# Masks of the prompt attention's scores: from TensorE products into VectorE's maximum

## The chip, the core and the metric

The kernel runs on one core of a Trainium2 chip. The metric is the device time of one execution in microseconds (us), the median over several runs. A core has five engines with a queue of instructions each: TensorE (PE; its weight loads are listed as PEld), VectorE (DVE), ScalarE (ACT), GpSimd (POOL) and SyncE (SP, which here only issues DMA transfers). Each engine takes its instructions in the order of the program and waits for the others by semaphores. Matrix products write to PSUM banks of 512 columns of fp32; everything else lies in SBUF.

## The reference

One layer of a decoder trunk runs for two groups: a prompt of 1024 tokens and a sample group of 8 sequences with 8 new tokens and 2048 cached ones each. A layer is half a SwiGLU feed-forward, a mixer and another half feed-forward. The mixer joins a Mamba-2 head group and an attention head group of 8 query heads over 2 key/value heads. The attention has three branches, compressed blocks, selected blocks and a sliding window of 512 tokens. With 1024 prompt tokens all 16 blocks are selected, so the prompt's selected branch is plain causal attention. Each branch is a masked softmax:

```python
def masked_softmax(s, mask):
    s = jnp.where(mask, s.astype(jnp.float32), NEG)
    e = jnp.where(mask, jnp.exp(s - jnp.max(s, axis=-1, keepdims=True)), 0.0)
    return e / jnp.maximum(jnp.sum(e, axis=-1, keepdims=True), 1e-30)
```

The selected branch masks keys after the query; the window branch masks those and keys 512 or more tokens back. Scores carry a slope times the distance (ALiBi) as well. For the sample group the compressed branch needs summaries of the cached rows: blocks of 32 rows go through a small two-layer network, per sequence, for keys and for values.

## The kernel before, in words

The program is one long function that goes through stages: first feed-forward, projections and Mamba-2, the prompt's attention (here from 1138 to 1548 us of the span), the sample group's attention together with the output projection (1548 to about 1740), second feed-forward, outputs. Products that need fp32 accuracy are split into high and low parts and made as three products.

**Prompt attention.** The loop goes over 8 tiles of 128 queries in the order `qt` = 2, 7, 6, 5, 4, 3, 1, 0, over two key/value heads g, over two branches br (0 selected, 1 window), and over the four query heads of g. The nk keys that a tile can see (up to 1024 in branch 0, up to 640 in branch 1) are taken in one part, or in two parts if they are more than 512. For a part of pn keys TensorE makes the scores s in one of three PSUM banks (`s2`) with two products, queries times keys (L1808) and ALiBi with the low parts (L1810). Then a mask product (L1813) adds the identity times a 128x128 tile of 0 and -1e30: `mdiag` on the last 128 keys of the last part, `medge` on the first 128 keys of the window when it is full (qt of 4 and more). The parts come to 192, the mask products to 160; 32 parts, the first of two in branch 0, have no mask. VectorE takes the maximum of a part (L1818 for one part; L1821 for each of two and L1822 over the two), and ScalarE makes the exponential from PSUM into the SBUF tile pb with the row sum beside it (L1824). There are five pb tiles per branch; a group of four heads uses four. After the four heads, pb is scaled by gate over sum (L275 to L279, on ScalarE, GpSimd or VectorE by a table), transposed by TensorE (L1846, pT), copied to SBUF (pt), and multiplied with the values into o (L1855). The compressed branch of the prompt (s_cmp, pc) has a mask product of its own (L1770), once per tile of queries.

**Compression of the sample group's cache.** Written between these tiles, by a table `cs` = 3, 0, 2, 1, 1, 0, 1, 0 that says how many sequences are started ahead of each tile of queries, and interleaved with them on all engines. For each of 8 sequences GpSimd issues a gather of the cached rows into chk (L1689, one buffer); then come eight steps of four transposes each: rows are put in order (chp, ScalarE and GpSimd), transposed (cT, L1712, one PSUM bank), split into high (th, ScalarE) and low (tl, VectorE, L1717), and multiplied with the weights w1h and w1l (cA, L1733 to L1735, 12 products per step). After four steps a summary is made (cxh, c).

**Sample attention.** It needs `big`, a tile of biases and constants that is loaded back from DRAM (L1951), the cached window rows (schk, loaded by SP, L2052), the cached selected blocks (schk, 32 gathers by GpSimd, L2048), the residual x (L1892) and w_out (raw, L1900). Their buffers take over SBUF space of the prompt's attention and of the compression. Its scores already use one VectorE instruction that adds a bias, takes the maximum and writes the sum to SBUF (L2080), followed by a read of the accumulator, and exponentials in place (L2090).

**What sets the order.** The order of each queue is made by the framework's scheduler from the order in the text and its own costs of the instructions; it isn't written by hand. An edit to one instruction can therefore move many others, on all engines.

Of the kernel before, what the change touches and what calls it, by code (L numbers as in the profile page):

```python
# [12 lines left out]
BF16 = mybir.dt.bfloat16  # L13
I32 = mybir.dt.int32
AF = mybir.ActivationFunctionType
OP = mybir.AluOpType
AX = mybir.AxisListType

P = 128
# [61 lines left out]
def hybrid_step(ctx: ExitStack, tc: tile.TileContext, *aps):  # L81
    nc = tc.nc
# [82 lines left out]
    identb = C.tile([P, P], BF16, name="identb")  # L165
# [1231 lines left out]
    KB = KV.tile([P, 2, 2, TP], F32R, name="KB")  # L1397
# [181 lines left out]
    Gs.close()  # L1579
    Ds = ExitStack()  # L1580
    AC = Ds.enter_context(pool("attc"))
    mdiag = AC.tile([P, P], BF16, name="mdiag")
    medge = AC.tile([P, P], BF16, name="medge")
    mcmp = AC.tile([P, 8, 64], BF16, name="mcmp")
    for t_ in (mdiag, medge, mcmp):
        nc.gpsimd.memset(t_, 0.0)
    nc.gpsimd.affine_select(out=mdiag, in_=mdiag, pattern=[[-1, P]], compare_op=OP.is_ge, fill=NEG,
                            base=0, channel_multiplier=1)
# [85 lines left out]
    with pool("att", bufs=2) as K, pool("att_ps2", bufs=3, space=PSUM) as PS2, \  # L1674
# [76 lines left out]
        for qi, qt in enumerate(KN["qt"]):  # L1751
# [3 lines left out]
            QBq = QBs[2 * (qi % 2):2 * (qi % 2) + 2]  # L1755
# [8 lines left out]
            s = PS2.tile([P, 512], F32, name="s_cmp", tag="s2")  # L1764
            for h in range(NH):
# [5 lines left out]
                             start=False, stop=True, skip_group_check=True)  # L1771
            sv = s.rearrange("p (h n) -> p h n", h=NH)
            mx = K.tile([P, NH], F32, name="mxc")
# [11 lines left out]
            for g in range(2):  # L1785
                PT = {}
                for br in range(2):
                    k0 = 0 if br == 0 else max(0, qt - 4)
                    nk = P * (qt + 1 - k0)
                    pbs = []  # L1790
                    hs_ = slice(4 * g, 4 * g + 4)
                    ns = (nk + 511) // 512
                    part = K.tile([P, 4, 2], F32, name="part", bufs=4)
                    for hh_ in range(4):
                        pb = K.tile([P, 1024 if br == 0 else 640], F32, name=f"pb{br}", bufs=5)
                        pbs.append(pb)
                        st, parts = 0, []
                        for i in range(ns):
                            pn = P * ((nk // P - st // P) // (ns - i))
                            s = PS2.tile([P, 512], F32, name="s2", tag="s2")[:, :pn]  # L1800
                            parts.append((s, st, pn))
                            kk = slice(P * k0 + st, P * k0 + st + pn)
                            masks = []
                            if st + pn == nk:
                                masks.append((pn - P, mdiag))
                            if br == 1 and qt >= 4 and st == 0:
                                masks.append((0, medge))
                            nc.tensor.matmul(s, QAs[g][:, hh_], KA[:, br, g, kk], start=True, stop=False,  # L1808
                                             skip_group_check=True)
                            nc.tensor.matmul(s, QBq[g][:97, hh_], KB[:97, br, g, kk], start=False, stop=not masks,  # L1810
                                             skip_group_check=True)
                            for j, (c, mk) in enumerate(masks):
                                nc.tensor.matmul(s[:, c:c + P], identb, mk, start=False,  # L1813
                                                 stop=(j == len(masks) - 1), skip_group_check=True)
                            st += pn
                        mx = K.tile([P, 3], F32, name="mx", bufs=4)
                        if ns == 1:
                            nc.vector.tensor_reduce(mx[:, 0:1], parts[0][0], axis=AX.X, op=OP.max, negate=True)  # L1818
                        else:
                            for i in range(2):  # L1820
                                nc.vector.tensor_reduce(mx[:, 1 + i:2 + i], parts[i][0], axis=AX.X, op=OP.max)  # L1821
                            nc.vector.tensor_reduce(mx[:, 0:1], mx[:, 1:3], axis=AX.X, op=OP.max, negate=True)  # L1822
                        for i, (s, st, pn) in enumerate(parts):
                            nc.scalar.activation(pb[:, st:st + pn], s, AF.Exp, bias=mx[:, 0:1],  # L1824
                                                 accum_out=part[:, hh_, i:i + 1])
                    total = part[:, :, 0]
                    if ns == 2:
                        total = sm[:, 1 + br, hs_]
                        nc.vector.tensor_tensor(total, part[:, :, 0], part[:, :, 1], op=OP.add)
                    nc.vector.reciprocal(sm[:, 1 + br, hs_], total)  # L1830
                    nc.vector.tensor_tensor(sm[:, 1 + br, hs_], sm[:, 1 + br, hs_],  # L1831
                                            gates[:, qt, 8 + 8 * br + 4 * g:12 + 8 * br + 4 * g], op=OP.mult)
                    for hh_ in range(4):
                        h, pb = 4 * g + hh_, pbs[hh_]
                        scale(KN["pb"][qi][4 * br + hh_], pb[:, :nk], pb[:, :nk], sm[:, 1 + br, h:h + 1])
                    PT[br] = (pbs, k0, nk // P)
# [696 lines left out]
```

## Time and profile before

| | us |
|---|---|
| median of 3 runs | 2470.73 (2468.52 to 2479.9) |
| the profiled execution | 2475.45, its span 2473.8 |
| TensorE / VectorE / ScalarE / GpSimd busy | 2408.8 / 1744.7 / 1131.2 / 418.3 |
| prompt attention, 1138 to 1548: TensorE / VectorE / ScalarE / GpSimd busy | 397.87 / 264.00 / 265.76 / 159.31 of 410 |
| mean granted clock of TensorE over the span | 0.987 |

The profile is of one execution, and its times are counted from the start of the span. Busy times of TensorE overlap, since its products are pipelined: a product of 256 columns is listed with 0.28 us while the next one starts 0.12 us later. What a product takes from the engine is therefore read from start to start. A wait is written as the waiting engine and line, an arrow, and the engine and line that released it.

### The profile page before, as it was taken

To read this page: it belongs to the slowest core of one execution; us is meant where nothing else is said; L and a number is where in the kernel's file an instruction comes from. 1 tells how busy PE (TensorE), PEld (TensorE's weight loads), DVE (VectorE), ACT (ScalarE), POOL (GpSimd) and SP (SyncE) were. 2 spreads that over 40 slices of the span, in tenths; PEclk is the share of its full clock that TensorE was granted. 3 is DMA by queue.
4 is the path that set the end of the run, shared out by engine and by line. 5 is a ranking of instruction groups with operands and counts; after the bars stand their busy time and mean duration, and the time that the engine had idled before them with its cause. 6 is when DMAs were issued, how large, how long until landed. Compare 5 with 4: busy or idle time off the path is not lost.

```text
span 2473.8 us, 48193 instructions
## 1 busy us (share of the span) xinstructions
PE 2408.8 (97%) x19026; PEld 2222.8 (90%) x19026; DVE 1744.7 (71%) x3673; ACT 1131.2 (46%) x2501; POOL 418.3 (17%) x533
## 2 busy tenths in 40 slices
PE   7999999999999999999999999999999999999998
PEld 6999999999999998997667766677899999999998
DVE  6777776677778855655656666777967676768776
ACT  7544444441133254425666675444545454543113
POOL 0000000011134343333434343111000000001110
PEclk9999999999999999999999998999999999999999
DMA  4334343598652333423110104476235353559654
GB/s 162 134 133 160 130 164 129 175 338 306 230 190 84 126 116 102 119 69 127 40 64 35 69 35 148 130 250 213 89 123 171 120 174 120 174 213 370 238 209 153
DMA packets 230446, 379.07 MB, mean 153 GB/s; under 512 B 18509, under 2 KB 147705, under 8 KB 228812
## 3 DMA queue, kind: packets, MB, share of 16 engines
q1 hardware_dynamic: 210248, 318.02, 37.7%
q0 software_dynamic: 7600, 38.59, 4.5%
q10 hardware_dynamic: 12372, 19.38, 2.2%
q8 instruction: 150, 2.46, 0.4%
q14 instruction: 76, 0.62, 0.1%
HBM read 255.66 MB, written 124.40 MB: 154 GB/s over the span
## 4 chain that ended last, share of the span: by engine, by line
PE 86%; DVE 6%; DMA 4%; ACT 3%; issue 1%; POOL 0%; ACTq 0%; DVEq 0%; POOLq 0%
PE dq L634 6%; PE gY L367 6%; PE dq L633 6%; PE dq L635 6%; PE gY L368 6%; PE gY L366 6%; PE gX L367 5%; PE gX L366 5%; PE gX L368 5%; PE o L1855 3%; PE pT L1846 3%; PE s L1808 1%; PE xbc L250 1%; PE xbc L251 1%; PE xbc L252 1%; PE cA L1733 1%
## 5 line engine op out<-in xcount | busy, mean ns | idle before, releaser
L634 PE MATMUL dq<-db,da 128*128 128x256 f32 (+1 forms) x1232 | 353.2, 288 | 0.3 <-DVE da L270 0.3
L635 PE MATMUL dq<-db,da 128*128 128x256 f32 (+1 forms) x1232 | 352.8, 288 | 0.0
L633 PE MATMUL dq<-db,da 128*128 128x256 f32 (+1 forms) x1232 | 349.8, 288 | 2.7 <-DVE Cc L386 2.2
L642 DVE TENSOR_TENSOR xT<-xT,dq 128x256 f32<-128x256 f32 (+1 forms) x456 | 186.9, 432 | 84.8 <-PE dq L635 83.2
L270 POOL TENSOR_TENSOR ds<-dw 128x512 f32<-128x512 f32 x22 | 29.5, 1341 | 1228.1 <-DVE wlo L270 508.0
L633 PEld LDWEIGHTS dq<-db,da 128*128 128x128 f32 x1232 | 230.5, 189 | 3.3 <-DVE Cc L386 2.5
L635 PEld LDWEIGHTS dq<-db,da 128*128 128x128 f32 x1232 | 232.8, 189 | 0.0
L634 PEld LDWEIGHTS dq<-db,da 128*128 128x128 f32 x1232 | 231.9, 188 | 0.6 <-DVE da L270 0.5
L267 ACT CAST whi<-ws 128x512 fp32r<-128x512 f32 x156 | 96.5, 623 | 205.9 <-PE gY L368 137.6
L270 DVE TENSOR_TENSOR wlo<-raw,whi 128x512 fp32r<-128x512 f32 x184 | 125.5, 687 | 83.9 <-ACT whi L267 83.5
L267 ACT CAST da<-ds 128x512 fp32r<-128x512 f32 x88 | 52.6, 623 | 234.7 <-PE dq L635 93.4
L267 ACT CAST whi<-raw 128x512 fp32r<-128x512 f32 x181 | 112.4, 626 | 72.0 <-PE g L414 19.5
L270 DVE TENSOR_TENSOR wlo<-ws,whi 128x512 fp32r<-128x512 f32 x156 | 106.7, 687 | 42.4 <-ACT whi L267 41.9
L1824 ACT ACTIVATE pb<-s,mx 128x256 f32<-128x256 f32 (+3 forms) x192 | 105.0, 552 | 59.7 <-DVE mx L1822 37.6
L1846 PEld LDWEIGHTS pT<-ident,pb 128*128 128x128 f32 x528 | 59.6, 143 | 45.8 <-issue 40.1
L1821 DVE TENSOR_REDUCE mx<-s 128x1 f32<-128x384 f32 (+2 forms) x128 | 66.6, 536 | 44.0 <-PE s L1813 34.1
L366 PE MATMUL gY<-B3h,whi 128*128 128x256 f32 (+1 forms) x320 | 91.5, 287 | 1.5 <-ACT whi L267 1.4
L366 PE MATMUL gX<-B6h,whi 128*128 128x256 f32 (+1 forms) x320 | 91.3, 286 | 0.9 <-ACT Cc L373 0.9
L367 PE MATMUL gX<-B6h,wlo 128*128 128x256 f32 (+1 forms) x320 | 91.4, 286 | 0.6 <-DVE wlo L270 0.6
L367 PE MATMUL gY<-B3h,wlo 128*128 128x256 f32 (+1 forms) x320 | 91.6, 287 | 0.2 <-DVE wlo L270 0.2
L277 POOL TENSOR_TENSOR pb<-pb,sm 128x640 f32<-128x640 f32 (+7 forms) x70 | 85.1, 1238 | 37.6 <-DVE sm L1831 34.0
L367 PE MATMUL gY<-B2h,wlo 128*128 128x256 f32 (+1 forms) x320 | 91.4, 286 | 0.0
(763 smaller groups left out, 8548.1 us busy)
## 6 DMA issues: line engine op xcount, KB each, us to landing
db<-GD SPq DMA_DIRECT2D x42, 1632.0 KB
GD<-Cc SPq DMA_DIRECT2D x154, 272.0 KB
GD<-his SPq DMA_DIRECT2D x84, 272.0 KB
raw<-in_ffn_wu_dram SPq DMA_DIRECT2D x22, 1024.0 KB
dw<-in_ffn_wd_dram SPq DMA_DIRECT2D x44, 512.0 KB
raw<-in_ffn_wg_dram SPq DMA_DIRECT2D x21, 1024.0 KB
GD<-hp SPq DMA_DIRECT2D x70, 272.0 KB
db<-GD SPq DMA_DIRECT2D x14, 1088.0 KB
```

The lines of the kernel that those rows point to most:

```text
L267: return nc.scalar.copy(out, src) if eng == "a" else ENGINES[eng].tensor_copy(out, src)
L270: ENGINES[eng].tensor_tensor(out, x, y, op=op)
L277: nc.gpsimd.tensor_tensor(out, x, by.to_broadcast(list(x.shape)), op=OP.mult)
L366: nc.tensor.matmul(q, ah[:, k], b_, start=first, stop=False, skip_group_check=True)
L367: nc.tensor.matmul(q, al[:, k], b_, start=False, stop=False, skip_group_check=True)
L368: nc.tensor.matmul(q, ah[:, k], c_, start=False, stop=(k == 3), skip_group_check=True)
L633: nc.tensor.matmul(q, x, bh[:, u, o], start=first, stop=False, skip_group_check=True)
L634: nc.tensor.matmul(q, y, bh[:, u, o], start=False, stop=False, skip_group_check=True)
L635: nc.tensor.matmul(q, x, bl[:, u, o], start=False, stop=(u == np_ - 1), skip_group_check=True)
L642: nc.vector.tensor_tensor(x, x, q, op=OP.subtract if i == 4 else OP.add)
L1824: nc.scalar.activation(pb[:, st:st + pn], s, AF.Exp, bias=mx[:, 0:1], accum_out=part[:, hh_, i:i + 1])
L1846: nc.tensor.transpose(tq_[:kn, P * hh_:P * hh_ + P], src, ident)
```

## The change

The tiles mdiag and medge become the two ends of one tile `mrow` of 640 columns with zeros between. A part that needs a mask gets a slice of it as wide as the part: the last pn columns for the last part of a tile, the first pn columns for the first part of a full window. The mask product is dropped, and the maximum of such a part is taken by VectorE's fused instruction, which adds the mask to the scores, writes the negated sum into pb and takes the minimum of it, the negated maximum. The exponential then reads pb and writes it in place with the scale -1. Parts without a mask keep the plain maximum and the exponential out of PSUM. Of two parts the smaller of the two negated maxima is taken.

```diff
-    mdiag = AC.tile([P, P], BF16, name="mdiag")
-    medge = AC.tile([P, P], BF16, name="medge")
+    mrow = AC.tile([P, 5 * P], BF16, name="mrow")
+    medge, mdiag = mrow[:, :P], mrow[:, 4 * P:]
...
-                            masks = []
+                            mask = None
                             if st + pn == nk:
-                                masks.append((pn - P, mdiag))
-                            if br == 1 and qt >= 4 and st == 0:
-                                masks.append((0, medge))
+                                mask = mrow[:, 5 * P - pn:]
+                            elif br == 1 and qt >= 4 and st == 0:
+                                mask = mrow[:, :pn]
...
-                            nc.tensor.matmul(s, QBq[g][:97, hh_], KB[:97, br, g, kk], start=False, stop=not masks,
+                            nc.tensor.matmul(s, QBq[g][:97, hh_], KB[:97, br, g, kk], start=False, stop=True,
                                              skip_group_check=True)
-                            for j, (c, mk) in enumerate(masks):
-                                nc.tensor.matmul(s[:, c:c + P], identb, mk, start=False,
-                                                 stop=(j == len(masks) - 1), skip_group_check=True)
+                            parts.append((s, mask, pb[:, st:st + pn]))
...
+                        for i, (s, mask, p_) in enumerate(parts):
+                            m_ = mx[:, 1 + i:2 + i] if ns == 2 else mx[:, 0:1]
+                            if mask is None:
+                                nc.vector.tensor_reduce(m_, s, axis=AX.X, op=OP.max, negate=True)
+                            else:
+                                nc.vector.tensor_tensor_reduce(out=p_, in0=s, in1=mask, scale=-1.0, scalar=3e38,
+                                                               op0=OP.add, op1=OP.min, accum_out=m_)
+                        if ns == 2:
+                            nc.vector.tensor_reduce(mx[:, 0:1], mx[:, 1:3], axis=AX.X, op=OP.min)
+                        for i, (s, mask, p_) in enumerate(parts):
+                            nc.scalar.activation(p_, s if mask is None else p_, AF.Exp, bias=mx[:, 0:1],
+                                                 scale=1.0 if mask is None else -1.0, accum_out=part[:, hh_, i:i + 1])
```

The scheduler gives the stage another order. Three places show it; numbers behind names are those of tiles, and `x2` stands for as many equal instructions in a row. First TensorE at the end of the prompt's attention, before: the last products o, and right behind them the sample group's first products.

```order
L1846 MATMUL pT<-ident,pc 64x128 x4
L1855 MATMUL o<-pt,VA 64x512 x2
L1855 MATMUL o<-pt,VAc 64x512
L1985 MATMUL a_ps<-gates,big 128x24
L2064 MATMUL kT_ps<-ident,schk 128x128 x8
```

After: the last products o, and behind them steps of the compression (the first of them are shown), then at their end the same first products.

```order
L1855 MATMUL o<-pt,VA 64x512 x2
L1855 MATMUL o<-pt,VAc 64x512
L1733 MATMUL cA<-th_13755,w1h 128x256
L1734 MATMUL cA<-th_13755,w1l 128x256
L1712 MATMUL cT<-ident,chp 128x128 x4
L1735 MATMUL cA<-tl_13756,w1h 128x256
...
L1743 MATMUL c_17967<-w_179,cxh 127x64 x2
L2096 LDWEIGHTS zrow
L2096 MATMUL so<-oneh,zrow 128x384
L2064 MATMUL kT_ps<-ident,schk 128x128 x8
```

Between the last o and the first kT_ps there now stand 132 products cA and 40 transposes cT, which were interleaved with the attention; before, the last cA stood ahead of the last 20 of the 192 score parts.

Second GpSimd in the same place, before: scalings of pb, the last reorderings chp, and the gathers of the selected blocks among the last scalings.

```order
L267 COPY chp<-chk 128x2x128 x3
L277 TENSOR_TENSOR pb_18160<-pb_18160,sm 128x256
L270 TENSOR_TENSOR pc<-pc,sm 128x512
L267 CAST QA<-QA 64x2x128
L270 TENSOR_TENSOR QB_13184<-qT,QA 64x2x128
L277 TENSOR_TENSOR pb_18199<-pb_18199,sm 128x256
L2048 DMA schk<-in_cache_sel_dram,idx_9814 128x1024
```

After: the last scaling of the whole stage, then the last gather of the compressed cache, its reorderings, and only then the selected blocks.

```order
L277 TENSOR_TENSOR pb_18405<-pb_18405,sm 128x128
L267 COPY chp<-chk 128x2x128
L1963 MEMSET QS 128x512
L1974 MEMSET zrow 32x128
L267 COPY chp<-chk 128x2x128
L1689 DMA chk<-in_cache_cmp_dram,idx 128x4096
L267 COPY chp<-chk 128x2x128 x8
L2048 DMA schk<-in_cache_sel_dram,idx_9814 128x1024 x32
```

The last gather L1689 moved from among the scalings of 640 columns to behind the last scaling of 128, and all 32 gathers L2048 stand behind it.

Third VectorE at a head with two parts, before: two maxima and the one over both, with a subtraction tl and a copy pt between them.

```order
L1821 TENSOR_REDUCE mx<-s_14710 128x1
L1717 TENSOR_TENSOR tl_13754<-cT,th_13753 128x2x256
L1822 TENSOR_REDUCE mx<-mx 128x1
L267 COPY pt<-pT 128x512
L1717 TENSOR_TENSOR tl_13758<-cT,th_13757 128x2x256
```

After, the same kind of head: the maximum of the part without a mask (L1817), the fused instruction of the other part, which is listed as ISA, and its read of the accumulator.

```order
L1817 TENSOR_REDUCE mx<-s_14689 128x1
L1819 ISA pb_14688,mx<-s_14692,mrow 128x512
L1819 ISA mx 128x1
L1822 TENSOR_REDUCE mx<-mx 128x1
L267 COPY pt<-pT 128x512
```

Every masked part now has two instructions on VectorE where there was one. On SP the order around the sample group's first loads is nearly the same, window rows first (L2052 twice), then big and x, with two tiles of w_out (L1900) now ahead of big.

More of the change, by code (lines that the diff above doesn't have):

```diff
@@ L1581, in hybrid_step @@
     AC = Ds.enter_context(pool("attc"))
-    mdiag = AC.tile([P, P], BF16, name="mdiag")
-    medge = AC.tile([P, P], BF16, name="medge")
+    mrow = AC.tile([P, 5 * P], BF16, name="mrow")
+    medge, mdiag = mrow[:, :P], mrow[:, 4 * P:]
     mcmp = AC.tile([P, 8, 64], BF16, name="mcmp")
-    for t_ in (mdiag, medge, mcmp):
+    for t_ in (mrow, mcmp):
         nc.gpsimd.memset(t_, 0.0)
@@ L1800, in hybrid_step @@
                             s = PS2.tile([P, 512], F32, name="s2", tag="s2")[:, :pn]
-                            parts.append((s, st, pn))
                             kk = slice(P * k0 + st, P * k0 + st + pn)
-                            masks = []
+                            mask = None
                             if st + pn == nk:
-                                masks.append((pn - P, mdiag))
-                            if br == 1 and qt >= 4 and st == 0:
-                                masks.append((0, medge))
+                                mask = mrow[:, 5 * P - pn:]
+                            elif br == 1 and qt >= 4 and st == 0:
+                                mask = mrow[:, :pn]
@@ L1815, in hybrid_step @@
                             st += pn
                         mx = K.tile([P, 3], F32, name="mx", bufs=4)
[L1817 to L1822, printed above, removed]
@@ L1823, in hybrid_step @@
-                        for i, (s, st, pn) in enumerate(parts):
-                            nc.scalar.activation(pb[:, st:st + pn], s, AF.Exp, bias=mx[:, 0:1],
-                                                 accum_out=part[:, hh_, i:i + 1])
+                        for i, (s, mask, p_) in enumerate(parts):
[5 more added lines that the diff above has]
+                                                               op0=OP.add, op1=OP.min, accum_out=m_)
```

## Prediction

> **What bounds the kernel now.** I read the page first, then the table by stretches of time, the waits and the chain of the prompt's attention (1138 to 1548 us), the only stage that the change edits, and last the timeline at its end. The page:
>
> ```profile
> span 2473.8 us, 48193 instructions
> PE 2408.8 (97%) x19026; PEld 2222.8 (90%) x19026; DVE 1744.7 (71%) x3673; ACT 1131.2 (46%) x2501; POOL 418.3 (17%) x533
> ```
>
> The table by stretches has the stretch, its length, the busy time of PE, PEld, DVE, ACT and POOL, the granted clock, the DMA share and GB/s: the whole stage, its end, and a later stretch of the sample group's attention.
>
> ```profile
> 1138.00:1548.00 410.00, 397.87 (x2645) 285.23 (x2645) 264.00 (x637) 265.76 (x717) 159.31 (x235) 0.98 0.18 67
> 1510.00:1548.00 38.00, 36.49 (x202) 23.09 (x201) 26.99 (x92) 20.84 (x73) 14.23 (x20) 0.82 0.70 257
> 1620.00:1660.00 40.00, 38.60 (x408) 29.54 (x408) 34.68 (x92) 20.33 (x39) 9.90 (x10) 1.00 0.89 293
> ```
>
> TensorE is busy for 398 of the stage's 410 us, VectorE for 264. So a product removed is worth about its own time, and work added to VectorE is paid only where TensorE comes to wait for it. The second row matters most: 257 GB/s are moved while the attention still runs. The waits of the stage (total us, times, longest) and what the loading queue waited for:
>
> ```profile
> ACT pb L1824 <- DVE mx L1822: 37.6, 37, 2.1
> ACT pb L1824 <- DVE mx L1818: 20.4, 21, 7.6
> PEld s L1808 <- ACT pb L1824: 8.5, 15, 0.9
> PE s L1808 <- ACT pb L1824: 3.8, 10, 0.7
> ACT pb L1824 <- PE pT L1846: 1.4, 2, 1.0
> ...
> SPq L2052 <- PE cA L1735: 382.6, 1, 382.6
> ```
>
> ScalarE waits 58 us for maxima and TensorE hardly ever for ScalarE (12.3 us). The last row is the one to keep: SP stands 382.6 us at L2052, the first cache-window load of the sample group, until the last product cA of the compressed cache. Everything queued on SP behind it waits with it. The chain of the stage, by line:
>
> ```profile
> by line: PE o L1855 19.2%; PE pT L1846 15.9%; PE s L1808 8.0%; PE cA L1733 6.9%; PE cA L1735 6.5%; PE s L1810 6.4%; PE cA L1734 6.3%; PE cT L1712 6.3%; DMA chk<-in_cache_cmp_dram,idx 4.9%; PE s L1813 2.2%; ACT pb L1824 2.0%; DVE mx L1821 1.
> ```
>
> The mask products (L1813) hold 2.2% of 410 us, 9.0 us. The gathers of the compressed cache (chk) hold 4.9%, 20 us: the chain of compression runs beside the attention and is nearly as late.
>
> **The masks, part by part.** Rows of the TensorE timeline (start, length) around three masks, then groups of instructions (count, busy us, mean ns); L2080 and L2090 are the sample group's code, which already has the form that the change brings in.
>
> ```profile
> 1222.43 0.29 PE L1810 MATMUL s<-KB,QB 97*128 97x256 f32 x1
> 1222.56 0.23 PE L1813 MATMUL s<-medge,identb 128*128 128x128 bf16 x1
> 1222.60 0.37 PE L1733 MATMUL cA<-th,w1h 128*128 128x256 f32 x1
> ...
> 1225.11 0.23 PE L1813 MATMUL s<-mdiag,identb 128*128 128x128 bf16 x1
> 1225.18 0.39 PE L1846 MATMUL pT<-ident,pb 128*128 128x128 f32 x2
> ```
>
> ```profile
> L1813 PE MATMUL s<-mdiag,identb 128*128 128x128 bf16 x128 | 30.1, 235 | 0.0
> L1813 PE MATMUL s<-medge,identb 128*128 128x128 bf16 x32 | 7.4, 232 | 0.0
> L1824 ACT ACTIVATE pb<-s,mx 128x512 f32<-128x512 f32 x40 | 27.2, 685 | 6.9 <-DVE mx L1822 3.6 <-DVE mx L1818 2.4 <-PE pT L1846 1.0
> L1821 DVE TENSOR_REDUCE mx<-s 128x1 f32<-128x512 f32 x24 | 16.2, 686 | 11.1 <-PE s L1813 8.0 <-PE s L1810 3.0
> L2080 DVE CUSTOM_DVE_ANT_0 S<-s_ps,big 128x512 f32<-128x512 f32 x20 | 13.7, 685 | 3.1 <-PE s_ps L2077 3.0
> L2080 DVE DVE_READ_ACCUMULATOR2_ANT smxs<- 128x1 f32 x20 | 1.7, 83 | 0.0
> L2090 ACT ACTIVATE S<-S,nm 128x512 f32<-128x512 f32 x12 | 8.6, 719 | 12.9 <-DVE nm L2089 12.9
> ```
>
> TensorE: 160 masks go. Start to start they take 0.04 us (1222.56 to 1222.60) or 0.07 us (1225.11 to 1225.18); 160 x 0.055 = 8.8 us, as the chain has it. The 37.5 us of the two mask rows are pipelined lengths, an upper end that is not reachable. **-8.8 us.**
>
> VectorE: the fused add and maximum takes 685 ns on 512 columns where the maximum alone takes 686, so only the accumulator read of 83 ns is new: 160 x 83 ns = 13.3 us on VectorE, which comes to 277 of 410 us. TensorE's products hide it; uncovered it would be the whole 13.3 us. The instruction now writes pb, so VectorE, not ScalarE, waits where a pb buffer is still being transposed (1.4 us before), and the copies of pT and subtractions of tl, for which TensorE's o and cA wait, queue behind. **0, at most +5 us.**
>
> ScalarE: exponentials read SBUF instead of PSUM, 719 against 685 ns; 160 x 34 ns = 5.4 us on an engine with 265.76 us busy. **0.** In return the PSUM bank of a masked part is free after VectorE, not after ScalarE. Of the 12.3 us that TensorE waits for ScalarE, the wait for VectorE's 0.69 us takes most back. **-4, between 0 and -12.**
>
> **What it moves.** The instruction order shows that the attention now runs ahead of the compression. Before, the last compression ends with 20 of the 192 score parts still to come; now the seventh sequence's last three steps and all of the eighth's eight steps (132 products cA, 40 transposes cT) stand behind the last product o. Rows of the last gather and of one step:
>
> ```profile
> 1453.43 9.67 DMA chk<-in_cache_cmp_dram,idx
> ...
> 1467.70 0.61 PE L1712 MATMUL cT<-ident,chp 128*128 128x128 f32 x4
> ```
>
> ```profile
> 1251.87 0.60 PE L1712 MATMUL cT<-ident,chp 128*128 128x128 f32 x4
> ...
> 1252.51 0.59 ACT L267 CAST th<-cT 128x512 fp32r<-128x512 f32 x1 [2.14 <-PE cT L1712]
> 1252.55 0.28 PE L1734 MATMUL cA<-th,w1l 128*128 128x256 f32 x1
> ...
> 1252.67 0.29 PE L1735 MATMUL cA<-tl,w1h 128*128 128x256 f32 x1
> ...
> 1253.13 0.69 DVE L1717 TENSOR_TENSOR tl<-cT,th 128x512 fp32r<-128x512 f32 x1
> ```
>
> A step goes cT, th, tl through a single PSUM bank: 1251.87 to 1253.82, with the next start some 2.05 us after the first. From gather to first transposes pass 14.3 us in company (1453.43 to 1467.70) and at least the transfer's 9.67; I take 12. The tail: one step until chk is free, 12 us, and nine steps' time for eight steps and the summary, 2.05 + 12 + 9 x 2.05 = 32.5 us. TensorE's work in it, which is moved and not new, is 132 x 0.12 (1252.55 to 1252.67) + 40 x 0.11 ((0.60 - 0.27)/3) = 20.2 us. **+12 us of idle TensorE; +8 with steps of 1.9 and a gather of 9.67, +30 if a step takes 4 us, half way to the 5.9 of the last sequence among attention work (1467.70 to 1514.59 below, over eight).** The attention in turn lacks this filling: **+3, between 0 and +10.**
>
> Then the start of the sample group. Rows where the compression ends and SP, then POOL, go on; landings (min, median, max) of schk; the size of big; products of the output projection; the first product that reads big, and the first of the sample's importance (range of starts at the end):
>
> ```profile
> 1514.59 0.28 PE L1735 MATMUL cA<-tl,w1h 128*128 128x256 f32 x1
> ...
> 1514.90 0.83 SPq L2052 DMA_DIRECT2D schk<-in_cache_win_dram  x2
> ...
> 1515.03 1.01 POOL L2048 DMA_INDIRECT schk<-in_cache_sel_dram,idx  x1 [1.55 <-PE cA L1735]
> ```
>
> ```profile
> DMA to landing us min/median/max: 4.2/6.0/12.3
> ```
>
> ```profile
> big<-saD SPq DMA_DIRECT2D x1, 2276.0 KB
> ```
>
> ```profile
> 1557.63 0.40 PE L251 MATMUL wout<-oh,wlo 128*128 128x512 f32 x1
> 1557.87 0.39 PE L252 MATMUL wout<-ol,whi 128*128 128x512 f32 x1
> ...
> L1985 PE MATMUL a_ps<-gates,big x8: 266/276/287, 1547.9 to 1671.8; 64*128 64x24 f32 x8
> L2006 PE MATMUL a_ps<-spc,big x8: 274/275/376, 1559.8 to 1681.8; 128*128 128x127 f32 x8
> ```
>
> Before, these loads start 33 us ahead of the stage's end and land under the attention. Now SP's window rows, w_out, big and x, and on POOL's queue all selected-block gathers (behind the last chk copies), start when the compression ends. TensorE's next product waits for schk: 6.0 less about 1 for the summary, +5. The split of w_out is late by some +1. Then 24 projection products of 0.24 us keep TensorE busy to about 14 us, while window rows, two w_out tiles and big (1.0 + 0.5 + 2.3 MB at 293 GB/s) take 13, +1. Behind big comes the sample's softmax, 11.9 us from L1985 to L2006 before, with filling that now is used up, +4. **+11 us, between 0 (later slack gives it back) and +24 (landings of 12.3, all of 11.9).**
>
> Sum: -8.8 - 4 + 3 + 12 + 11 = +13. The profiled execution took 2475.45 us, its span 2473.8; that is 4.7 above the median of 2470.73. It would become 2488.5, the median 2484.
>
> **Rivals.** 0.5% of the median is 12.4 us, about what a measurement of this kernel can tell from no change.
>
> A, the forecast: tail and late loads outweigh the masks: 2484, itself 2475 to 2494.
>
> B, the start-up is absorbed: the stage after has waits of its own, and engines that cast and split during the tail are ahead later. For it: the tail leaves VectorE and ScalarE nearly free. Against it: 257 GB/s were needed under the attention. Without the +11: 2473.
>
> C, the other side: TensorE counts alone. The freed banks give all of 12.3, the body loses nothing, the tail costs the short +8, loads are hidden: -8.8 - 12.3 + 8 = -13, and of the clock's loss at the end of the stage ((1 - 0.82) x 38 = 6.8 us) some 3 goes: 2455. It decides if the last cA comes before about 1530 us; the order speaks against it.
>
> D, the tail runs cold. The clock of 0.82 in the 1510 row shows that a thinly filled end loses clock; a gather wait with TensorE empty is thinner. At half clock the 20.2 us of work take twice that, and a step 3.8 us of TensorE instead of a 2.05 us loop: 8 x 1.75 = 14 us more, 2498. It decides from some steps above 3 us.
>
> The Trainium skill, "TensorE: Matmul & The Clock Gate", Part 1, says that the array falls to half clock after an idle window of about 3.4 us and returns after a busy one. By that rule the gather wait gives D, at least for its first steps; the trace agrees in the row of 0.82 as far as it goes, and no wait as long as this one stands in it.
>
> **How the numbers follow.** A 0.50, B 0.20, C 0.09, D 0.21. The range from 2460 to 2509 takes in A, B and most of D and leaves out C and D's worst. Slower by over 0.5% (above 2483): half of A and all of D, 0.46; faster (below 2458): C, 0.09; within: B and the other half of A, 0.45.
>
> **What would show it.** Right: no L1813; 160 fused instructions of 685 ns at 512 columns with reads of 83 ns; the last cA some 30 us after the last o; a gap of TensorE of 6 us or more during the last chk gather; schk, big and w_out issued only after that; PE busy in the stage below 97%. Wrong: a fused instruction much longer than the maximum; the end of the compression under the attention; TensorE waiting mostly for VectorE's mx all through the stage, which would put the cost into the body and not at its end.

## The result, and the profile after

The changed kernel took 2494.3 us (median of 6 runs, 2490.24 to 2500.59), the kernel before 2472.34 us (6 runs, 2468.52 to 2479.9). The ratio is 1.009 with a 95% interval of 1.0071 to 1.0108: slower by 0.9%, 22 us. The profiled execution took 2493.86 us, its span 2490.6. Below, a ratio is turned into us by 2472.

The page of the changed kernel, its first lines:

```profile
span 2490.6 us, 48039 instructions
PE 2398.1 (96%) x18866; PEld 2221.8 (89%) x18866; DVE 1750.8 (70%) x3833; ACT 1134.6 (46%) x2501; POOL 419.0 (17%) x532
```

160 products fewer on TensorE, 160 instructions more on VectorE, as the change says. VectorE's groups of the stage show what the new instructions take, by shape (count, busy us, mean ns, idle time before them):

```profile
L1819 DVE CUSTOM_DVE_ANT_0 pb<-s,mrow 128x384 f32<-128x384 f32 x64 | 34.6, 550 | 6.4 <-PE pT L1846 4.3 <-PE s L1809 1.7
L1819 DVE CUSTOM_DVE_ANT_0 pb<-s,mrow 128x512 f32<-128x512 f32 x32 | 21.5, 686 | 6.0 <-PE s L1809 4.0 <-PE pT L1846 1.8
L1819 DVE DVE_READ_ACCUMULATOR2_ANT mx<- 128x1 f32 x160 | 13.1, 82 | 0.0
```

TensorE's share of the stage (1138 to 1548 us) is below the 97% of before, 386.75 of 410 us:

```profile
1138.00:1548.00 410.00, 386.75 (x2513) 286.02 (x2511) 274.89 (x810) 274.76 (x724) 157.49 (x237) 0.97 0.14 51
```

A fused part of 512 columns takes 686 ns and its read 82 ns, as forecast from the sample group's instructions. Where the time went is seen from the products that begin and end each piece. The tile views give count, ns (least, middle, most), and first and last start; of the kernel before:

```profile
L1808 PE MATMUL s<-KA,QA x192: 277/406/580, 1138.3 to 1537.4; 128*128 128x384 f32 x80, 128*128 128x256 f32 x56, 128*128 128x512 f32 x40, 128*128 128x128 f32 x16
L1855 PE MATMUL o<-pt,VAc x32: 589/640/1109, 1162.3 to 1547.4; 64*64 64x512 f32 x32
L1735 PE MATMUL cA<-tl,w1h x256: 277/282/562, 1157.1 to 1514.6; 128*128 128x256 f32 x128
L2064 PE MATMUL kT_ps<-ident,schk x160: 270/273/476, 1548.2 to 1710.5; 128*128 128x128 f32 x160
L252 PE MATMUL wout<-ol,whi x192: 288/296/628, 1556.9 to 1753.3; 128*128 128x288 f32 x128, 128*128 128x512 f32 x64
```

And of the changed kernel:

```profile
L1807 PE MATMUL s<-KA,QA x192: 273/365/793, 1140.5 to 1500.0; 128*128 128x384 f32 x80, 128*128 128x256 f32 x56, 128*128 128x512 f32 x40, 128*128 128x128 f32 x16
L1855 PE MATMUL o<-pt,VAc x32: 589/614/641, 1167.3 to 1506.0; 64*64 64x512 f32 x32
L1735 PE MATMUL cA<-tl,w1h x256: 277/282/562, 1158.2 to 1540.9; 128*128 128x256 f32 x128
L2064 PE MATMUL kT_ps<-ident,schk x160: 270/273/476, 1545.1 to 1730.1; 128*128 128x128 f32 x160
L252 PE MATMUL wout<-ol,whi x192: 288/297/628, 1559.4 to 1769.6; 128*128 128x288 f32 x128, 128*128 128x512 f32 x64
```

Read the two side by side. From the first score product to the first kT_ps, which is the prompt's attention with the whole compression, before took 409.9 us and the change 404.6: the stage that the change edits became 5.3 us **shorter**, though its compression now ends 34.9 us behind the last o. From the first kT_ps to the last wout, in code that the change does not touch, before took 205.1 us and the change 224.5: 19.4 us **longer**. Behind that, both take about as long (720.5 and 721.0 us of span), and the changed stage began 2.2 us later, which adds up to the 16.8 us by which the spans of the two profiles differ. So the loss lies in the sample group's stage, and its waits stand at the start of it: in the first 30 us from the first kT_ps on, the waits listed for TensorE's products come to 12.1 us in the change and to 1.4 before. Rows of the changed kernel's timeline where the compression ends:

```profile
1540.92 0.28 PE L1735 MATMUL cA<-tl,w1h 128*128 128x256 f32 x1
1541.23 0.83 SPq L2052 DMA_DIRECT2D schk<-in_cache_win_dram  x2
...
1544.74 0.34 SPq L1951 DMA_DIRECT2D big<-saD  x1
...
1545.11 2.32 PE L2064 MATMUL kT_ps<-ident,schk 128*128 128x128 f32 x8 [1.46 <-DMA schk<-in_cache_win_dram]
```

SP's first load starts 0.3 us after the last cA, when TensorE has little else left. SP's wait row says the same:

```profile
SPq L2052 <- PE cA L1735: 407.2, 1, 407.2
```

The table by stretches of the changed kernel (stretch, length, busy us of PE, PEld, DVE, ACT, POOL, granted clock, which is the mean share of its full clock that TensorE got, DMA share, GB/s) through its tail and the start behind it:

```profile
1506.00:1520.00 14.00, 8.18 (x54) 6.52 (x52) 6.38 (x16) 5.76 (x13) 1.87 (x4) 0.90 0.40 150
1520.00:1530.00 10.00, 9.39 (x62) 8.77 (x63) 2.85 (x5) 4.09 (x10) 1.95 (x5) 0.80 0.01 2
1530.00:1541.00 11.00, 8.96 (x68) 7.62 (x66) 3.40 (x6) 3.44 (x8) 1.75 (x3) 1.00 0.17 48
1541.00:1550.00 9.00, 5.19 (x19) 2.34 (x17) 0.71 (x2) 2.06 (x4) 6.57 (x7) 0.69 0.87 315
1550.00:1558.00 8.00, 0.87 (x3) 0.29 (x1) 0.69 (x1) 0.91 (x2) 0.00 (x0) 0.50 1.07 430
1558.00:1566.00 8.00, 7.62 (x29) 5.82 (x29) 1.57 (x4) 0.33 (x1) 0.00 (x0) 0.78 1.01 386
1566.00:1574.00 8.00, 3.80 (x25) 2.69 (x23) 6.20 (x20) 1.52 (x5) 0.00 (x0) 0.65 0.44 138
```

And the same place of the kernel before:

```profile
1548.00:1556.00 8.00, 6.64 (x28) 3.67 (x29) 7.02 (x22) 6.64 (x15) 0.00 (x0) 0.67 0.32 97
1556.00:1564.00 8.00, 8.00 (x41) 6.43 (x40) 5.47 (x17) 3.02 (x7) 0.00 (x0) 0.91 0.42 125
1564.00:1572.00 8.00, 8.00 (x48) 5.70 (x46) 7.06 (x11) 2.30 (x4) 0.00 (x0) 1.00 0.12 35
```

In the change the DMA engines are full (share 1.07, 430 GB/s) while TensorE does 0.87 us of work in 8; before, TensorE never stands idle like that, with at most 125 GB/s to move, and it is at full work and full clock 16 us after the first kT_ps. The long waits of TensorE in that gap, and behind it what ScalarE and VectorE waited for between 1541 and 1590 us:

```profile
1553.85 0.80 PE L250 MATMUL wout<-oh,whi 128*128 128x512 f32 x1 [3.77 <-ACT whi L267]
...
1558.38 0.79 PE L250 MATMUL wout<-oh,whi 128*128 128x512 f32 x1 [3.73 <-ACT whi L267]
...
1569.16 0.77 PE L2006 MATMUL a_ps<-spc,big 128*128 128x127 f32 x2 [2.67 <-DVE spc L2003]
```

```profile
ACT whi L267 <- DMA raw<-in_w_out_dram: 9.0, 2, 5.1
...
DVE S L2080 <- DMA big<-saD: 4.2, 1, 4.2
```

TensorE waits for splits of w_out tiles, and the splits for the tiles' loads; behind them comes big, and the softmax that needs it.

### The profile page after: what moved, and what is told of

The parts are those of the page before. It is cut to its first block, busy times and chain, and to the rows that moved or that the text cites. A ratio compares the mean times of both kernels' runs of the same rounds, so it can differ in the third digit from the quotient of the medians.

```text
span 2490.6 us, 48039 instructions
## 1 busy us (share of the span) xinstructions
PE 2398.1 (96%) x18866; PEld 2221.8 (89%) x18866; DVE 1750.8 (70%) x3833; ACT 1134.6 (46%) x2501; POOL 419.0 (17%) x532
## 4 chain that ended last, share of the span: by engine, by line
PE 84%; DVE 7%; DMA 4%; ACT 2%; issue 2%; POOL 0%; SPq 0%; ACTq 0%; DVEq 0%; POOLq 0%
PE gY L367 6%; PE gY L368 6%; PE gY L366 6%; PE dq L634 6%; PE dq L633 6%; PE dq L635 6%; PE gX L367 5%; PE gX L366 5%; PE gX L368 5%; PE o L1855 3%; PE pT L1846 3%; PE s L1807 1%; PE xbc L250 1%; PE xbc L251 1%; PE xbc L252 1%
## 5 line engine op out<-in xcount | busy, mean ns | idle before, releaser
L1824 ACT ACTIVATE pb<-pb,mx 128x384 f32<-128x384 f32 (+3 forms) x160 | 92.1, 576 | 28.8 <-DVE mx L1819 22.4
L1819 DVE CUSTOM_DVE_ANT_0 pb<-s,mrow 128x384 f32<-128x384 f32 (+3 forms) x160 | 78.4, 511 | 19.8 <-PE s L1809 9.9
```

The costliest lines, as they stand in the source:

```text
L1824: nc.scalar.activation(p_, s if mask is None else p_, AF.Exp, bias=mx[:, 0:1], scale=1.0 if mask is None else -1.0, accum_out=part[:, hh_, ...
```

## The experiments

The theory: the change's instructions cost about nothing, and the loss is the order that the scheduler gives them, by way of the late loads. The main rival: the cost is in the body (VectorE's reads, in-place exponentials). All twelve variants were compared with the kernel before on the same chip. The lead is the time from the last cA, which lets the loads start, to the first kT_ps; the stage runs from the first s to the first kT_ps, the start from there to the last wout, both in us of the profiled execution (the stage of late_loads holds the wait that it puts in).

| kernel | masks added by | median us (before) | ratio, 95% interval | stage | lead | start |
|---|---|---|---|---|---|---|
| before | TensorE | 2472.3 | | 409.9 | 33.6 | 205.1 |
| changed | VectorE | 2494.3 (2472.3) | 1.0090, 1.0071 to 1.0108 | 404.6 | 4.2 | 224.5 |
| paced | VectorE | 2472.4 (2472.2) | 0.9997, 0.9987 to 1.0007 | 407.0 | 28.4 | 203.9 |
| late8 | TensorE | 2526.2 (2472.2) | 1.0215, 1.0199 to 1.0231 | 436.5 | 4.0 | 229.4 |
| late_same | TensorE | 2527.8 (2471.0) | 1.0214, 1.0198 to 1.0229 | 437.2 | 3.9 | 229.5 |
| both | both | 2499.5 (2471.9) | 1.0106, 1.0083 to 1.0128 | 404.5 | 3.9 | 229.1 |
| late_loads | TensorE | 2496.4 (2471.9) | 1.0094, 1.0074 to 1.0113 | 418.9 | – | 214.1 |
| paced_mid | VectorE | 2483.7 (2471.9) | 1.0047, 1.0032 to 1.0063 | 406.3 | 11.6 | 213.3 |
| early2 | VectorE | 2498.0 (2471.0) | 1.0101, 1.0085 to 1.0117 | 426.9 | 81.2 | 206.6 |
| fused_ps | both | 2481.9 (2472.2) | 1.0031, 1.0017 to 1.0044 | 414.5 | 23.7 | 205.6 |
| nomask | nobody | 2476.0 (2472.2) | 1.0015, 1.0006 to 1.0024 | 403.7 | 37.7 | 212.2 |
| nomask_ord | nobody | 2473.8 (2471.0) | 1.0012, 1.0001 to 1.0023 | 404.0 | 37.5 | 206.2 |
| paced_ord | VectorE | 2474.2 (2471.0) | 1.0008, 0.9997 to 1.0019 | 403.8 | 25.8 | 205.5 |
| more_masks | TensorE | 2509.2 (2471.9) | 1.0136, 1.0114 to 1.0159 | 439.3 | 40.5 | 205.7 |

**paced: the change with the old order.** On the changed kernel; `ends` holds each sequence's last cA product:

```diff
+PACE = (29, 49, 67, 86, 107, 129, 150, 172)
-nc.tensor.matmul(s, QAs[g][:, hh_], KA[:, br, g, kk], start=True, stop=False, ...)
+sc = nc.tensor.matmul(s, QAs[g][:, hh_], KA[:, br, g, kk], start=True, stop=False, ...)
+for e_, at in zip(ends, PACE):
+    if at == count:      # the count-th score part stands behind that cA in TensorE's queue
+        tc.add_manual_dep(sc.ins, e_.ins.name, <order only>)
+count += 1
```

> The changed kernel with its instructions untouched, but eight score products held, in TensorE's queue alone, behind the last compression product (cA) of one sequence each, at the places where these ended in the kernel before (29, 49, 67, 86, 107, 129, 150, 172 of 192 score parts). Theory (the loss is the order: compression behind the attention, loads of the sample group behind the compression): the order cost goes and the masks' gain of 5 to 13 us shows, 2460 to 2467 us, last cA at 1500 to 1515, first schk load by 1516. Rival 1 (the cost is in the body: fused instructions with accumulator reads on VectorE, in-place exponentials): stays at 2488 to 2496. Rival 2 (the products removed were hidden, so the change has nothing to give): 2470 to 2475.

Measured 2472.4 us: the 22 us are gone with not one instruction changed. The loss is the order; the body rival falls. But the masks' gain did not show either, and in that rival 2 was right. Its rows:

```profile
L2072 PE MATMUL kT_ps<-ident,schk x160: 270/273/476, 1545.2 to 1707.0; 128*128 128x128 f32 x160
L252 PE MATMUL wout<-ol,whi x192: 288/297/487, 1553.9 to 1749.1; 128*128 128x288 f32 x128, 128*128 128x512 f32 x64
```

The paced kernel reaches the first kT_ps at 1545.2 us, the changed one at 1545.1. They part only behind that: 203.9 against 224.5 us. These 20.6 us are the difference between the two kernels: the spans of the two profiles (2490.6 and 2473.3 us) differ by 17.3, since the changed one is 3.2 us shorter behind the last wout.

**late8 and late_same: the old instructions in the new order.** late8 holds, in the kernel before, the seventh sequence's last three steps and the eighth sequence behind the last o; late_same holds each of the 64 steps where the change has it. Both hold TensorE's queue alone, and the held sequences are written behind the loop, so the other engines' queues need not have the order of the change. The edit of late_same:

```diff
-    compress_sample(next(sequences))
+    pass                                  # all eight are emitted behind the loop
+    tc.add_manual_dep(<first transpose of step n>, <score product PACE[n]>, <order only>)
```

> The kernel before, masks by TensorE, with only the order of the change put on it: the seventh sequence's last three compression steps and the whole eighth sequence stand behind the last product o. Theory (order costs all): the time after plus the masks' 9 us, 2497 to 2508, with a tail of 35 to 40 us from last o to the first kT_ps. Rival 1 (the body of the change costs): the order alone costs little, 2470 to 2480. Rival 2 (the late order is cheap because the compression is then denser; the loss comes of the combination with freed banks): 2480 to 2488.

> The kernel before, masks by TensorE, with each of the 64 compression steps held behind the score product behind which it stands in the changed kernel (TensorE's queue alone), so that the last two sequences end behind the last product o. Theory (the order alone costs the 22 us, the paced run showed that the change's instructions cost nothing): 2492 to 2502. Rival 1 (the late order is cheap with masks on TensorE): 2472 to 2484. Rival 2 (without banks freed early the attention can't run ahead without loss, as in the late8 run): 2510 to 2530.

Measured +53 us both: more than any expectation of late8, and what rival 2 of late_same expected. The start is 229 us, near the change's 224.5; what is new is the stage, 437 us against the change's 404.6. So with masks on TensorE and the exponential reading PSUM, this order of TensorE loses in the attention as well. That the banks held until ScalarE has read them are the cause is rival 2's argument, and these runs do not show it. Two of TensorE's waits of late_same, and the one in their place in the change:

```profile
PE s L1811 <- ACT pb L1827: 7.7, 13, 1.3
PEld s L1811 <- ACT pb L1827: 11.6, 19, 1.6
```

```profile
PE s L1807 <- DVE mx L1819: 4.7, 7, 2.2
PEld s L1807 <- DVE mx L1819: 8.6, 15, 2.4
```

The waits of products differ by 3.0 us and those of weight loads, which overlap them, by 3.0, so they do not account for the 32.6 us by which the stages differ. Against `both` below, which has all mask products too, late_same takes 18.6 us longer from the first s to the last o (394.6 against 376.0 us); TensorE is idle for 18.2 of them against 7.2, and its granted clock is 0.98 against 1.00.

**both: the change with the mask products kept.**

```diff
+masks = [(pn - P, mdiag)] if st + pn == nk else []
+...
+for j, (c, mk) in enumerate(masks):
+    nc.tensor.matmul(s[:, c:c + P], identb, mk, start=False, stop=(j == len(masks) - 1), ...)
```

> The changed kernel with the 160 mask products kept as well (masks are added twice). The scheduler gives it the late order of the change by itself. Theory (the late order costs the kernel before 56 us and the changed one 22 because VectorE frees the PSUM banks early, not because products are gone): 2494 to 2503. Rival (what makes the late order dense is that the products and their weight loads are gone): 2515 to 2530.

Masks are added twice here. Measured 2499.5 us, as the theory had it; the stage takes 404.5 us, as in the change, with all products kept. So it is not fewer products that make the late order bearable. late_same, without the fused, in-place form, took 1.0214 against 1.0106, some 27 us more. That points to the form, but does not show it alone: 132 products cA stand behind the last o in late_same and in the change, 96 in `both`, and the other queues of late_same are not those of `both`. The form also brings a late order about: in its instruction order `both`, which keeps all mask products, has the last cA behind all 192 score parts, while fused_ps below, whose exponentials still hold the bank, has it behind 178 (before: 172).

**late_loads: late loads and nothing else.** On the kernel before; every load of the first group carries

```diff
+tc.add_manual_dep(dma.ins, last_o.ins.name, <waits for it>)   # schk, big, x rows, w_out
```

> The kernel before, its compression as early as ever, but the first loads of the sample group (cache-window rows and first selected blocks into schk, big, x rows, w_out tiles) held until the last product o. Theory (the late start of these loads is what the change loses: the changed and the paced kernel reach the first kT_ps at the same 1545.1 us, and part by 20.6 us up to the last product wout): 2486 to 2497. Rival (a late start is absorbed by slack in the stage after): 2471 to 2478.

Measured +23 us by the ratio, inside the theory's range. The compression ended as early as ever (1517.2 us). From last o to last wout it took 226.5 us against 205.9 before, 20.6 us longer, and a gap opens like the one in the change; the rows of the last o and the last wout, then the stretches:

```profile
L1855 PE MATMUL o<-pt,VAc x32: 589/614/640, 1165.6 to 1546.2; 64*64 64x512 f32 x32
L252 PE MATMUL wout<-ol,whi x192: 290/296/628, 1573.0 to 1772.7; 128*128 128x288 f32 x128, 128*128 128x512 f32 x64
```

```profile
1546.00:1554.00 8.00, 1.10 (x3) 0.09 (x1) 4.53 (x12) 2.91 (x6) 5.36 (x6) 0.82 0.78 290
1554.00:1562.00 8.00, 3.09 (x13) 2.20 (x14) 1.97 (x8) 1.08 (x3) 2.31 (x3) 0.50 0.99 398
1562.00:1570.00 8.00, 3.19 (x17) 1.22 (x16) 4.11 (x11) 0.59 (x1) 0.00 (x0) 0.71 1.05 400
```

TensorE does 7.4 us of work in 24, with the DMA engines nearly full. So a late start of these loads, by itself, costs as much as the change does. The gap has other parts, though: SP issues big first here, so TensorE waits 8.9 us for big and then 5.6 us for a split of w_out.

**paced_mid and early2: between the orders, and beyond the old one.** The paced kernel with other places: (33, 52, 76, 101, 127, 151, 170, 184), and (16, 32, 48, 66, 84, 102, 120, 140) with the sequences emitted earlier to match.

> The changed kernel with the compression held between the two orders: its sequences end at 33, 52, 76, 101, 127, 151, 170 and 184 of 192 score parts (before 172, in the change behind the last). Theory (the attention is denser when it may run ahead, and the loads of the sample group, which start about 1520 to 1525, still land under its end): 2463 to 2472. Rival (each us of later loads is lost): 2475 to 2485.

> The changed kernel with the compression held earlier still: its sequences end at 16, 32, 48, 66, 84, 102, 120 and 140 of 192 score parts, so the first loads of the sample group can start some 35 us before they did in the kernel before. Theory (in the paced run these loads are hidden already, so earlier is worth nothing more, and the end of the attention lacks the compression as filling): 2472 to 2482. Rival (every us of earlier load is a gain): 2455 to 2465.

paced_mid: +12 us, the theory's forecast missed and the rival's met. Its loads start 11.6 us ahead, and its start takes 213.3 us, half way. With the other rows of the table: leads of 24 us and more give starts of 204 to 207 us (nomask, whose later order differs, aside), 12 us give 213, 4 us give 225 to 229. early2: +25 us, worse than either expectation. Its loads are hidden (206.6 us); its stage takes 426.9 us, 20 more than the paced one. With the compression gone from its end, TensorE waits longer for maxima; early2's rows, then the paced kernel's:

```profile
PE s L1810 <- DVE mx L1827: 12.5, 16, 4.1
PEld s L1810 <- DVE mx L1827: 22.3, 33, 4.3
```

```profile
PE s L1810 <- DVE mx L1827: 7.7, 11, 2.0
PEld s L1810 <- DVE mx L1827: 14.6, 26, 2.2
```

These rows hold a part of the 20 us: products wait 4.8 us longer for maxima, and TensorE's idle time in all grows by 11.5 us (30.4 us of 426.0 in early2, 18.9 of 406.1 in paced). So the old order, early enough for the loads and late enough to fill the attention, beat both neighbours that were tried.

**nomask, more_masks, fused_ps: the prices of the parts.** nomask is the kernel before without its 160 mask products (the masks of the window and selected scores are left out). more_masks puts four products with a zero tile ahead of each mask. fused_ps is the kernel `both` with exponentials that read PSUM again:

```diff
-nc.scalar.activation(p_, s if mask is None else p_, AF.Exp, bias=mx[:, 0:1], scale=1.0 if mask is None else -1.0, ...)
+nc.scalar.activation(p_, s, AF.Exp, bias=mx[:, 0:1], scale=1.0, ...)
```

> The kernel before without its 160 mask products (it leaves the masks of the prompt's window and selected scores out), order otherwise as before. TensorE's pipelined issue as priced in the prediction (0.055 us each): -9 us, 2461 to 2466. If the products' full pipelined length of 0.235 us counted: -37, 2435. If they were hidden: no change, 2470 to 2475. The distance from this run to the paced one is what the fused instructions and in-place exponentials cost or give: theory 0 to -4 us, body rival +13.

> The kernel before with four products of a zero tile ahead of each mask product, into the same columns: 640 products more, the result unchanged. Removing 160 gave nothing to the whole. If TensorE's issue bounds the attention at 0.055 us a product: 35 us, 2500 to 2512. If such products are hidden beside the other waits of the stage: 2470 to 2480.

> Masks stay on TensorE, VectorE adds them a second time in the fused maximum (its sum is thrown into pb and overwritten), the exponential still reads PSUM: 160 accumulator reads and writes of pb more than the kernel before, its PSUM banks as long held, its order nearly that of before (the compression ends at 178 of 192 parts). Theory: VectorE's work is hidden, 2470 to 2478. Body rival: VectorE's 13.3 us of reads show, 2483 to 2490.

more_masks: 640 products more cost 34 us by the ratio (28 to 39), 0.053 us each, as their issue in the timeline says. In its profile the stage is 29.4 us longer, 0.046 us each, at a granted clock of 1.00 against 0.98 before; 8.0 us more lie ahead of the first s, where no product was added, and stay unexplained. nomask: 160 fewer gave nothing, and rather cost 4 us (1.5 to 5.9). In its profile the stage is 6.2 us shorter, and this gain is lost in the sample group's stage (212.2 us against 205.1). fused_ps: +8 us by the ratio, between the two expectations. Its stage is 4.6 us longer than before, so VectorE's reads and writes of pb seem not to be wholly hidden where the bank stays held; its order is not quite that of before (the last cA behind 178 score parts, not 172), so the two are not told apart.

**nomask_ord and paced_ord: the later order held too.** All 7002 products behind the last o were put into the order of the kernel before:

```diff
+for x, y in zip(order_, order_[1:]):
+    tc.add_manual_dep(EM[y], EM[x].name, <order only>)
```

> The kernel before without its mask products (the masks of the prompt's window and selected scores are left out), and with TensorE's 7002 products behind the last product o held in the order of the kernel before. In the run without masks the stage ended 6 us earlier, and kept 6.9 us for as long as TensorE's order was that of before (its first 387 products after the stage); the lead went in the stretch where the order differs (1670 to 1720 us). Theory (the new order there ate it): the lead stays to the end, 2464 to 2467. Rival (a load or an engine of the sample group's attention bounds its end, whatever the order): 2471 to 2477.

> The paced run (all instructions of the change, compression as early as before) with TensorE's 7002 products behind the last o held in the order of the kernel before. The paced profile was 3 us ahead at the first kT_ps and 0.4 us at the end. Theory (later order ate it): 3 us are kept, 2467 to 2470, the first version below the kernel before. Rival (a bound of the later stage takes it): 2471 to 2474.

In the profiles it did what it should: starts of 206.2 and 205.5 us, stages 6 us shorter than before, and times of 2468.99 and 2469.69 us for these executions against 2475.45 for the profiled one of before (nomask_ord owes 3.4 us of that to a stage that began earlier, at 1134.9 us). But the medians of 12 runs are 2473.8 and 2474.2 us: no faster than before, where the rivals had them (paced_ord 0.2 us above its range). The later order is thus not enough to explain the missing gain, and no bound in the later stage shows in these profiles either. What can be seen of the other executions is their mean granted clock: 0.9864 and 0.9872 on average over 12 runs, and 0.9889 over the 23 of before beside them (nomask 0.9847, paced 0.9857, before 0.9881). A lower clock goes with the missing gain. Whether it causes it, and why it falls, stays open. No version beat the kernel before.

## Why the prediction was right, and where not

The forecast was 2484 us, case A; it came to 2494.3, inside the range but at the upper end of A's own 2475 to 2494. The mechanism held: a compression behind the attention, loads behind the compression, and that outweighs the masks. Of the sum of +13 us, profile against profile +18.4 came (2493.86 less 2475.45). That the sum came so near is in part luck, because two misses of 13 us cancel. Up to the last o the terms (-8.8, -4, +3 and 20.2 us of work moved away) give 30 us less, and 43.6 less came (365.5 us against 409.1). The tail and the wait for the first landing were forecast at 37.5 us, and 39.1 came. Behind the first kT_ps 6 us were forecast (+1, +1, +4), and 19.4 came. By its steps:

- **Masks, -8.8.** The issue time was about right (0.046 to 0.053 us each when added, 0.055 forecast), the gain was not: the stage without them is 6.2 us shorter in the profile, the time of the whole kernel not shorter at all (nomask, nomask_ord). The step "a product removed is worth about its own time" fails for the whole kernel.
- **VectorE's reads, 0, and banks, -4.** Together they gave about nothing. With the later order held, nomask_ord and paced_ord differ by reads and freed banks: 1.0012 against 1.0008, within their intervals, and stages of 404.0 and 403.8 us. (nomask and paced differ by 4.4 us in paced's favour by the ratios, but paced's stage is the longer one, 407.0 us against 403.7, and behind it their orders differ.) fused_ps has the reads at up to +8 us, 4.6 of them in its stage, so if the two add, the banks give some -5 to -9, within their range; no run shows them apart. In the late order up to 27 us stand between late_same and both, which no bound of the prediction had. The sums of waits (12.3 us before, 13.3 after) add products and weight loads, which overlap; of products alone it is 3.8 us before and 4.7 after.
- **ScalarE, 0.** The exponentials in place took 715 ns at 512 columns, against 685 out of PSUM and 719 forecast, and no run shows a cost of them.
- **Attention without its filling, +3, and tail, +12.** From last o to first kT_ps 39.1 us passed, 32.5 forecast for the tail, the last cA 34.9 us behind the last o where 30 was named. TensorE was about as idle in it as forecast, 11.5 us (8.5 of them in the 35 us up to 1541), but not in the way forecast: no wait of 6 us or more came during the last gather, since the seventh sequence's steps filled part of it (the longest is 1.73 us, below). And the attention ahead of the tail was faster, as said above: the sum had the stage some 7 us longer with masks, banks and the first landing, and it became 5.3 us shorter. Where these 13 us come from was not taken apart.
- **Start of the sample group, +11.** This is the mis-sized term. The wait for schk, forecast at 5, took 1.46 us; what lies behind it, forecast at 6, took 19.4 us (20.6 against the paced kernel), and 20.6 came in late_loads. The bound of 24 holds them together. The step that failed is "The split of w_out is late by some +1", and with it "keep TensorE busy to about 14 us": the 24 projection products were to cover the landing of big, but w_out itself lands late, so TensorE waits 3.77 and 3.73 us for its splits first, and then 2.67 us for the softmax. Of the 19.4 us, listed waits explain 12.1 less the 1.4 before. TensorE's clock was at 0.50 for some 27 us there (about 1544.5 to 1561.6 and 1568.4 to 1578.6 us), against some 7 before (1550.7 to 1557.5); what that costs was not taken apart.
- **Rival B** (start absorbed, 2473) falls: nothing was given back behind the last wout. **C** (2455) falls by its own mark: last cA at 1540.9, not before 1530. **D** (a cold tail, 2498) is the nearest in time, and its mechanism came in part. The 0.90 and 0.80 of the tail's rows are means: from about 1517.2 to 1524.0 us the granted clock was 0.50, and the eighth sequence's first transposes took 1.11 us (below), where 0.60 to 0.66 are listed later in the tail at 1.00. But of the 14 us that D added, TensorE's 4.6 us of work in that time can explain some 2 (an estimate: half of it), so D is not what made the time. The clock fell to 0.50 again at the start of the sample group.

The rows for the tail, its longest wait and its sum:

```profile
1518.66 1.11 PE L1712 MATMUL cT<-ident,chp 128*128 128x128 f32 x4 [1.73 <-ACT chp L267]
```

```profile
1506.00:1541.00 35.00, 26.53 (x182) 22.91 (x180) 12.63 (x26) 13.29 (x29) 5.57 (x11) 0.90 0.22 76
```

By the Trainium skill, "TensorE: Matmul & The Clock Gate", Part 1, an idle window of about 3.4 us puts the array at half clock. This trace shows the fall without a single wait of that length. The two waits of 3.7 us stand in the row of 0.50, but the clock had fallen ahead of them, at about 1544.5 us, behind a wait of 1.56 us and within one of 1.46, with TensorE busy for 1.1 us from 1541 to 1545. In the tail it fell at about 1517.2 us, and no listed wait ahead of it in the tail is above 1.6 us. The row of 0.82 of the kernel before, in which the prediction saw the trace agree, is a mean too: about 24 us at 1.00 and 14 at 0.50, with no listed wait of TensorE's products above 0.7 us.

Of the signs named as right, the gap of 6 us is the one that did not come. Of those named as wrong, none came: the fused instruction takes 686 ns, and TensorE's products wait 4.7 us for mx in the changed kernel, about the 3.8 us that they waited for ScalarE before.

## What to carry to other kernels

When a change lets buffers go earlier, look at what the scheduler does with that before pricing instructions: here the same instructions cost 22 us in the scheduler's order and nothing in another. A load that waits on the last use of reused SBUF has its start set by that last use, so give that chain a finishing time with enough lead for the loads to land (24 us were enough here, 12 were not). Then hold the order by explicit edges at a few places, neither later nor much earlier, since work that fills another stage's waits is missed there.

## What the runs showed of the hardware

- At the start of the changed sample group the DMA engines are full, share 1.07 and 430 GB/s, while TensorE's granted clock is 0.50 and its busy time 0.87 us in 8; its long waits there are for splits of w_out tiles, and these wait 9.0 us for the tiles' loads.
- The granted clock fell to 0.50 behind stretches of short waits: 1.1 us of work in 4 (1541 to 1545 us, waits of at most 1.6 us), and 4.1 us of work in 8 (1509 to 1517 us, waits of at most 1.6 us).
- Executions of one kernel spread over 11 us, and the mean granted clock goes with it: among the 23 of before beside late_same, 2465.49 us at 0.992 and 2477.02 us at 0.986.
- 640 added products of 128 columns cost about their issue time (34 us by the ratio, 29.4 in their stage), 160 removed ones gave none back to the whole.
